# The opening of a two-layer hybrid trunk as a list of steps, with 28 identity products ahead of it, moved gate steps, and a later bias sum

## The chip, the cores and the metric

One core of a Trainium2 chip runs the whole program. The metric is the device time of one execution in microseconds (us); lower is better. The kernel before takes 2284.15 us (median of 3 runs, 2282.27 to 2289.24). The engines are called by the profile's names: PE is TensorE's matmul stream and PEld its weight loads, DVE is VectorE, ACT is ScalarE, POOL is GpSimd, SP is SyncE, which issues all large transfers.

## What is computed

The input is a sequence of 1024 rows of 1024 numbers, a conditioning vector c and integer positions. Layer A is a matrix-memory mixer (mLSTM) and a squared-ReLU MLP, layer B latent attention and an MLP. Cut to what the change touches:

```python
c_act = silu(c)
sh1, sc1, g1, sh2, sc2, g2 = split(c_act @ mod_w[layer] + mod_b[layer], 6)
h = rms_norm(x, g) * (1 + sc1) + sh1                   # modulate
q, k, v, o_pre, i_pre, f_pre = split(h @ w_in, idx)    # layer A's projections
bc = cumsum(log_sigmoid(f_pre))                        # gates, per chunk of the recurrence
y = (sigmoid(o_pre) * rms_norm(hh, head_norm)) @ w_out # hh: what the mLSTM gives
x = x + g1 * rms_norm(y)                               # residual
ckv, k_rope = split(modulate(rms_norm(x), shift, scale) @ w_dkv)   # layer B's latent K/V
qa = modulate(rms_norm(x), sh1, sc1) @ w_qa            # layer B's latent q
cos, sin = rope_tables(positions)
```

All of it is float32. A product of two matrices is made of three TensorE products of rounded parts: each factor is split into a high part (`whi`, `hTh`, `uh`, `tbh`, a copy on ACT) and a remainder (`wlo`, `hTl`, `ul`, `tbl`, a subtraction on DVE), and `mm3` adds high x high, remainder x high and high x remainder (lines 168, 169 and 170 before).

## The kernel before

The sequence is cut into eight tiles of 128 rows (`tb`), the model width into eight slices of 128 columns (`k`). The kernel writes instructions in program order; a scheduler with a timeline model then sets the order on each engine, within the dependences, the tile pools, and pins that the kernel writes by hand: `self.behind(PE, V, S)` puts what follows behind the last instruction so far of these engines, and `issue_after` behind one given instruction. All large tiles (raw weights, their parts, activations, slabs, modw rows) come from one pool of 52 units, and a transfer waits on SP until its unit is free. PSUM has two double tiles `MM` (1024 columns) and four single ones `SM` (512 columns).

**The opening** makes the first half of layer A: the first four tiles of x are normed, transposed (`transposes`, L208: TensorE products with the identity), modulated and split, and meet two groups of weights: the first of the three pieces of v with the gate columns (`value(k)`, four tiles of 344 columns, 12 products per k) and the first two heads of q (`query(h, k)`, 3 products of 512 columns per k). The modulation needs shift and scale columns, c_act @ mod_w. They come two slices at a time from a slab of mod_w (slabs 0, 2, 4, 6, each in four units): for slab 0 as a row on TensorE (`mod_row`, L1040) that ACT copies, for slabs 2, 4 and 6 as sums of eight multiples on DVE (`mod_sum`, L1030 and L1032); small TensorE products with a column of ones (`mod_cols`, L1051) then turn them into columns, and `turned` transposes x and modulates (L985 on ACT, L987 on DVE). The order of these steps is written as nested `behind` blocks. In it the four value sums live in SM tiles, the transposed x and the two heads in the two MM tiles.

**After the opening** come the second half of the first two pieces, with the late constants (`lcols`, 32 columns transposed from small rows), then the rope tables (`rope_tables`, from `posi`, cast to `posf`, transposed), and the gates (`gates`, a generator: each `yield` lets other work be written in between; L1337 and L1352 are its TensorE steps between DVE ones). Beside them run the modulation vectors for later (`mods`, one accumulation of a modw row per step, L290 and L292, then `column`: eight transposes of `acc`).

**The mLSTM's end** makes sigmoid of the output gates (L1231, ACT) and multiplies it by `headg`, a slice of `lcols`.

**Layer B's latent projections** are made beside layer A's second MLP half. Their weights are scaled by the modulation's scale when they are split; the shift's part is a bias row: DVE adds up shift x weight (`lbias`, L1549), and one product with a matrix of ones (L1552) sums it over the partitions and spreads it, written at the end of the split of each of the two weights (320 and 384 columns). `latent_mix` makes the two projections of a tile and adds the bias (L1579). The MLP's residual adds there are on POOL (L445).

Of the kernel before, what the change touches and what calls it, by code (L numbers as in the profile page):

```python
# [13 lines left out]
AF = mybir.ActivationFunctionType  # L14
# [7 lines left out]
P = 128  # L22
# [43 lines left out]
class Trunk:  # L66
# [144 lines left out]
    def consts(self):  # L211
# [11 lines left out]
        self.transposes(ps, [crow])  # L223
        c = self.C("ccol", [P, KD])
# [28 lines left out]
    def late_consts(self):  # L253
# [20 lines left out]
        self.headg = self.lcols[:, 8:16]  # L274
# [668 lines left out]
    def layer_a(self):  # L943
# [60 lines left out]
        xs, slabs, sums, accs = [], [], {}, {}  # L1004
# [17 lines left out]
        def mod_sum(k, r0=0, r1=KD):  # L1022

            if r0 == 0:
                accs[k] = self.U("acc")[:, : 4 * P].rearrange("p (s c) -> p s c", s=2)
            acc = accs[k]
# [6 lines left out]
            for j in range(2):  # L1033
                sums[k + j] = acc[:, :, j * P : (j + 1) * P]

        def mod_row(k):

            ps = self.SM()
            for i in range(KD):
                PE.matmul(ps[0:1].rearrange("p (s c) -> p s c", s=2), self.cact[:, i : i + 1], slab_part(k, i), start=i == 0, stop=i == KD - 1)  # L1040
            row = self.U("acc")[0:1, : 4 * P]
            S.copy(row, ps[0:1])
            for j in range(2):
                sums[k + j] = row.rearrange("p (s c) -> p s c", s=2)[:, :, j * P : (j + 1) * P]

        def mod_cols(k, ps):

            for j in range(2):
                acc = sums.pop(k + j)
                for s in range(2):  # L1050
                    PE.matmul(ps[:, 2 * s + j : 2 * s + j + 1], acc[:, s], self.ones[: acc.shape[0], 0:1], start=True, stop=True)  # L1051
# [5 lines left out]
        def turned(k):  # L1057

            for j in range(2):
                ps = turn[:, j * 512 : j * 512 + 512]  # L1060
                if j == 0:
                    mod_cols(k, turn[:, 512:])
                self.transposes(ps, [x[:, (k + j) * P : (k + j + 1) * P] for x in xs[:4]])
                modulate(k + j, ps, self.U("t")[:, :512], *hT_part(0, k + j, slice(0, 512)), True)
# [34 lines left out]
        w, wq, acc = [], [], [None] * 4  # L1099

        def value(k):
            for tb in range(4):
                if k == 0:
                    acc[tb] = self.SM()
# [3 lines left out]
        def query(h, *ks):  # L1108
            for k in ks:
                c = tuple(u[:, k * P : (k + 1) * P] for u in wq[h])  # L1110
                self.mm3(heads[:, h * 512 : h * 512 + 512], c, self.hT_half(hT, 0, k), k == 0, k == KD - 1)

        normed(xs[:4], 2)
        with self.behind(V, S):
            w.append(self.take(("v", 0, 0)))
            with self.behind(V, S):
                mod_sum(2, 0, 2)
                mod_row(0)
                turn, heads = self.MM(), self.MM()
                with self.behind(V):  # L1120
                    turned(0)
        mod_sum(2, 2)
        wq.append(self.take(("q", 0)))
        value(0)
        with self.behind(PE, V, S):
            turned(2)
        with self.behind(PE, V, S):
            value(1)
            w.append(self.take(("v", 0, 1)))
            wq.append(self.take(("q", 1)))  # L1130
            with self.behind(V):
                mod_sum(4)
            value(2)
            value(3)
        with self.behind(PE, V, S):
            turned(4)
        with self.behind(PE, V, S):
            query(0, 0, 1, 2, 3)
            query(1, 0, 1, 2, 3)
            w.append(self.take(("v", 0, 2)))  # L1140
            with self.behind(V):
                mod_sum(6)
            value(4)
# [833 lines left out]
```

## Time and profile before

| what | before |
|---|---|
| median of 3 runs | 2284.15 us (2282.27 to 2289.24) |
| profiled execution's own time | 2283.3 us |
| its span | 2281.5 us |
| PE busy | 2199.2 us (96%) |
| DVE busy | 1693.9 us (74%) |
| ACT busy | 1031.2 us (45%) |
| POOL busy | 473.2 us (21%) |
| opening, to the first product of v's second piece | 74.04 us |

The span is what lies between the first and the last instruction of one profiled execution; some 2 us of its time lie around it. A row of the waits names the instructions that waited, by engine, tile and line, and the instruction whose end released them, then the total, the number and the longest of these waits. A row of the windows gives one stretch: its length, then for each engine the busy time and in brackets the instructions, the granted clock of TensorE (1.00 is full), the share of the DMA engines and GB/s. A row of the groups gives line, engine, operation, tiles and shapes, number, then busy time and mean ns of one, then idle time before them. A row of the timeline gives start, duration, engine, line and tiles; matmuls overlap, so a duration there is longer than the distance to the next.

### The profile page before, as it was taken

To read this page: it belongs to the slowest core of one execution; us is meant where nothing else is said; L and a number is where in the kernel's file an instruction comes from. 1 tells how busy PE (TensorE), PEld (TensorE's weight loads), DVE (VectorE), ACT (ScalarE), POOL (GpSimd) and SP (SyncE) were. 2 spreads that over 40 slices of the span, in tenths; PEclk is the share of its full clock that TensorE was granted. 3 is DMA by queue.
4 is the path that set the end of the run, shared out by engine and by line. 5 is a ranking of instruction groups with operands and counts; after the bars stand their busy time and mean duration, and the time that the engine had idled before them with its cause. 6 is when DMAs were issued, how large, how long until landed. Compare 5 with 4: busy or idle time off the path is not lost.

```text
span 2281.5 us, 28823 instructions
## 1 busy us (share of the span) xinstructions
PE 2199.2 (96%) x10746; PEld 1833.2 (80%) x10746; DVE 1693.9 (74%) x2496; ACT 1031.2 (45%) x1708; POOL 473.2 (21%) x317
## 2 busy tenths in 40 slices
PE   6999999999999999999999999999999999999998
PEld 4988888887778877777799989988787888777776
DVE  5577687667987767878978676664678877687888
ACT  3421367564444464333344544555734444633322
POOL 0000110004543333331011000000054433333300
PEclk7999999999999999999999999999999999999999
DMA  8287443234874464454322000022357645545452
GB/s 297 71 271 261 152 131 120 88 107 131 260 237 152 153 196 145 134 171 132 123 75 59 13 17 12 29 84 102 110 158 229 193 141 189 171 134 160 130 173 104
DMA packets 300068, 320.16 MB, mean 140 GB/s; under 512 B 16041, under 2 KB 252185, under 8 KB 299929
## 3 DMA queue, kind: packets, MB, share of 16 engines
q1 hardware_dynamic: 299928, 318.33, 44.2%
q8 instruction: 84, 1.38, 0.2%
q14 instruction: 56, 0.45, 0.1%
HBM read 245.85 MB, written 72.43 MB: 140 GB/s over the span
## 4 chain that ended last, share of the span: by engine, by line
PE 77%; DVE 14%; ACT 3%; issue 3%; DMA 3%; SPq 1%; POOL 0%; DVEq 0%; ACTq 0%; POOLq 0%
PE mm L168 14%; PE mm L169 14%; PE mm L170 14%; PE sm L168 10%; PE sm L170 9%; PE sm L169 9%; PE sm L208 3%; DVE wlo L598 2%; DVE ul L807 2%; DVE y L813 2%; DMA modw<-in_mod_w_dram 1%; DVE x L733 1%; DVE y L879 1%; DVE acc L292 0%; PE mm L1847 0%
## 5 line engine op out<-in xcount | busy, mean ns | idle before, releaser
L168 PE MATMUL mm<-whi,uh 128*128 128x512 f32 x688 | 273.7, 398 | 15.4 <-DVE y L813 15.1
L169 PE MATMUL mm<-wlo,uh 128*128 128x512 f32 x688 | 271.0, 394 | 0.0
L170 PE MATMUL mm<-whi,ul 128*128 128x512 f32 x688 | 270.5, 394 | 0.0
L813 DVE TENSOR_TENSOR y<-y,mm 128x1024 f32<-128x1024 f32 (+1 forms) x161 | 192.6, 1208 | 84.9 <-PE mm L170 84.8
L625 POOL TENSOR_TENSOR tt<-raw,tt 128x512 f32<-128x512 f32 x60 | 113.6, 1893 | 610.2 <-DVE wlo L598 610.2
L168 PE MATMUL sm<-hSh,whi 128*128 128x512 f32 x560 | 221.8, 396 | 9.2 <-DVE x L733 9.2
L169 PE MATMUL sm<-hSl,whi 128*128 128x512 f32 x560 | 220.4, 394 | 0.0
L170 PE MATMUL sm<-hSh,wlo 128*128 128x512 f32 x560 | 219.3, 394 | 0.0
L733 DVE TENSOR_TENSOR x<-x,sm 128x512 f32<-128x512 f32 x198 | 132.3, 682 | 55.9 <-PE sm L170 52.9
L168 PEld LDWEIGHTS mm<-whi,uh 128*128 128x128 f32 x688 | 129.1, 188 | 55.2 <-DVE y L813 22.7
L807 DVE TENSOR_TENSOR ul<-u,uh 128x896 fp32r<-128x896 f32 (+1 forms) x120 | 153.5, 1318 | 24.8 <-ACT uh L801 24.8
L605 POOL TENSOR_TENSOR tt<-raw,raw 128x512 f32<-128x512 f32 x32 | 63.9, 1997 | 488.8 <-ACT x L740 456.9
L801 ACT CAST uh<-u 128x896 fp32r<-128x896 f32 (+1 forms) x120 | 109.6, 948 | 122.1 <-DVE ul L807 114.0
L170 PEld LDWEIGHTS mm<-whi,ul 128*128 128x128 f32 x688 | 129.2, 188 | 30.2
L169 PEld LDWEIGHTS mm<-wlo,uh 128*128 128x128 f32 x688 | 129.2, 188 | 28.9
L598 DVE TENSOR_TENSOR wlo<-raw,whi 128x1024 fp32r<-128x1024 f32 x104 | 147.6, 1420 | 5.6 <-ACT whi L594 5.6
L168 PEld LDWEIGHTS sm<-hSh,whi 128*128 128x128 f32 x560 | 105.1, 188 | 36.7 <-DVE x L733 7.9
L736 ACT ACTIVATE x<-x 128x1024 f32<-128x1024 f32 x64 | 67.8, 1059 | 143.3 <-DVE x L733 143.2
L594 ACT CAST whi<-raw 128x1024 fp32r<-128x1024 f32 x104 | 108.7, 1046 | 43.7 <-DMA raw<-in_ffn_w_dram 21.5
L170 PEld LDWEIGHTS sm<-hSh,wlo 128*128 128x128 f32 x560 | 105.1, 188 | 25.0
L169 PEld LDWEIGHTS sm<-hSl,whi 128*128 128x128 f32 x560 | 105.2, 188 | 24.2
L292 DVE SCALAR_TENSOR_TENSOR acc<-modw,cact,acc 128x1024 f32<-128x1024 f32 x84 | 114.5, 1363 | 5.3 <-DMA modw<-in_mod_w_dram 3.7
(423 smaller groups left out, 5751.9 us busy)
## 6 DMA issues: line engine op xcount, KB each, us to landing
raw<-in_ffn_w_dram SPq DMA_DIRECT2D x144, 512.0 KB
u<-us SPq DMA_DIRECT2D x112, 448.0 KB
us<-x SPq DMA_DIRECT2D x92, 512.0 KB
modw<-in_mod_w_dram SPq DMA_DIRECT2D x80, 512.0 KB
x<-xn SPq DMA_DIRECT2D x24, 512.0 KB
x<-x SPq DMA_DIRECT2D x24, 512.0 KB
x<-in_x_dram SPq DMA_DIRECT2D x16, 512.0 KB
slab<-in_mod_w_dram SPq DMA_DIRECT2D x32, 256.0 KB
```

The source lines that it names most:

```text
L168: mm(out, a[0], b[0], start=start, stop=False)
L169: mm(out, a[0], b[1], start=False, stop=False)
L170: mm(out, a[1], b[0], start=False, stop=stop)
L208: self.PE.transpose(out[: s.shape[-1], j * P : j * P + s.shape[0]], s, self.ident[: s.shape[0], : s.shape[0]])
L292: self.V.scalar_tensor_tensor(out=acc, in0=t, scalar=self.cact[:, k : k + 1], in1=acc, op0=ALU.mult, op1=ALU.add)
L594: S.copy(x[0], u)
L598: V.tensor_tensor(out=x[1], in0=u, in1=x[0].bitcast(F32), op=ALU.subtract)
L625: G.tensor_tensor(out=t1, in0=b21, in1=t2, op=ALU.subtract)
L733: V.tensor_tensor(out=dst, in0=src, in1=ps, op=ALU.add)
L801: S.copy(x[0], u)
L807: V.tensor_tensor(out=x[1], in0=u, in1=x[0].bitcast(F32), op=ALU.subtract)
L813: V.tensor_tensor(out=dst, in0=dst, in1=ps, op=ALU.add)
```

## The change

Six things are changed.

1. Behind the transposition of c's row, 28 products of the identity with itself are written into an SM tile that nothing reads.
2. The opening becomes one list of steps, each pinned behind the one before on PE, VectorE and ScalarE. In it two of the eight rows of slab 2 are summed on TensorE (`mod_row, 2, 6`), so that `sums[2]` has two accumulators; `mod_sum` is cut into pieces with other steps between; transposing (`turn`) and modulating (`made`) are separate steps; weight splits are steps. The value sums live in the MM tiles, the heads and the transposed x in SM tiles. Two raw weights are kept ahead instead of three afterwards (`early`).
3. The rope tables are written before the second half of v's first piece, not after it. `mod_steps` begins inside that loop, and `gates` has two more `yield`s and starts beside the second half of the first head.
4. The sigmoid of the output gates is written as 0.5 (1 + tanh(x/2)): ACT makes tanh, DVE adds 1 and multiplies by `headg`, which is now half of the slice of `lcols`. The number of activation table loads in ACT's stream goes from 20 to 6.
5. The product that sums `lbias` is written in `latent_mix`, behind the products of the first tile's projection that needs it, and no longer in the split of the weight.
6. The eight residual adds in layer A's MLP go from POOL to VectorE.

The core of the diff:

```diff
         self.transposes(ps, [crow])
+        busy = self.SM()
+        with self.behind(self.PE):
+            for _ in range(28):
+                self.PE.matmul(busy[:, :P], self.ident, self.ident, start=True, stop=True)
...
-        self.headg = self.lcols[:, 8:16]
+        self.headg = self.C("headg", [P, KD])
+        self.V.tensor_scalar(out=self.headg, in0=self.lcols[:, 8:16], scalar1=0.5, scalar2=None, op0=ALU.mult)
...
+        def mod_row(k, r0=0, r1=KD):
+            ps = self.SM()[0:1]
+            for i in range(r0, r1):
+                PE.matmul(ps.rearrange("p (s c) -> p s c", s=2), self.cact[:, i : i + 1], slab_part(k, i), start=i == r0, stop=i == r1 - 1)
+            row = self.U("acc")[0:1, : 4 * P]
+            S.copy(row, ps)
+            sums[k].append(row.rearrange("p (s c) -> p s c", s=2))
+        def mod_cols(k):
+            ps = self.SM()
             for j in range(2):
                 for s in range(2):
+                    for i, acc in enumerate(sums[k]):
+                        PE.matmul(
+                            ps[:, 2 * s + j : 2 * s + j + 1], acc[:, s, j * P : (j + 1) * P], self.ones[: acc.shape[0], 0:1],
+                            start=i == 0, stop=i == len(sums[k]) - 1,
+                        )
...
+        def turn(*ks):
+            for k in ks:
+                turned[k] = self.SM()
+                self.transposes(turned[k], [x[:, k * P : (k + 1) * P] for x in xs[:4]])
+        def made(k):
+            modulate(k, turned.pop(k), self.U("t")[:, :512], *hT_part(0, k, slice(0, 512)), True)
...
+        both = [self.MM() for _ in range(2)]
+        acc = [both[tb // 2][:, tb % 2 * 512 : tb % 2 * 512 + 512] for tb in range(4)]
...
+        for step in (
+            (mod_row, 0), (mod_cols, 0), (turn, 0, 1), (split_v, 0), (mod_sum, 2, 0, 2), (made, 0), (mod_sum, 2, 2, 4), (made, 1),
+            (value, 0), (mod_row, 2, 6), (value, 1), (mod_sum, 2, 4, 6),
+            (mod_cols, 2), (turn, 2, 3), (split_q, 0), (split_v, 1), (query, 0, 0, 1), (made, 2), (split_q, 1), (made, 3),
+            (value, 2), (mod_sum, 4), (value, 3), (query, 0, 2, 3), (query, 1, 0, 1),
+            (mod_cols, 4), (turn, 4, 5), (split_v, 2), (query, 1, 2, 3), (mod_sum, 6, 0, 3), (made, 4), (mod_sum, 6, 3, 5), (made, 5),
+            (value, 4), (value, 5), (mod_sum, 6, 5), (query, 0, 4, 5),
+            (mod_cols, 6), (turn, 6, 7), (query, 1, 4, 5), (made, 6), (made, 7),
+            (value, 6), (value, 7), (query, 0, 6, 7), (query, 1, 6, 7),
+        ):
+            with self.behind(PE, V, S):
+                step[0](*step[1:])
...
-        self.ahead, self.early = 3, 3
+        self.rope_tables()
+        self.ahead, self.early = 3, 2
...
         for tb in range(4, NT):
             values(tb, proj_piece(w, tb))
+            if tb > 4:
+                mod_steps(2)
+        steps = self.gates(gi, gf)
         for h in range(2):
+            next(steps)
             put_qk("q", q, h, 1, self.proj_half(self.SM(), wq[h], hT, 1))
-            next(steps)
-            mod_steps(3)
...
-                S.activation(dst, ps[:, pr * 256 : (pr + 1) * 256], AF.Sigmoid)
-                V.tensor_scalar(out=dst, in0=dst, scalar1=self.headg[:, j : j + 1], scalar2=None, op0=ALU.mult)
+                S.activation(dst, ps[:, pr * 256 : (pr + 1) * 256], AF.Tanh, scale=0.5)
+                V.tensor_scalar(out=dst, in0=dst, scalar1=1.0, scalar2=self.headg[:, j : j + 1], op0=ALU.add, op1=ALU.mult)
...
-                    if k0 + nk == KD:
-                        ps = self.SM()
-                        PE.matmul(ps[:, :n], self.ones, bias, start=True, stop=True)
-                        S.copy(bias, ps[:, :n])
...
+            if o not in self.lb:
+                bias = self.lb["bias"][:, o : o + n]
+                total = self.SM()
+                with self.tc.issue_after(self.last()):
+                    self.PE.matmul(total[:, :n], self.ones, bias, start=True, stop=True)
+                self.S.copy(bias, total[:, :n])
+                self.lb[o] = bias
...
-            xn = self.residual(y, st["g"], st["x"].pop(tb), self.G)
+            xn = self.residual(y, st["g"], st["x"].pop(tb))
```

What that does to the order of instructions is shown at three places; the line numbers of the changed kernel differ from those of before.

TensorE's first rows in the changed kernel (crow is c's row, rows the norm weights and biases, slab the first slab of mod_w, acc_275 ACT's copy of the row of sums, x_126 the first tile of x):

```order
L208 MATMUL sm_82<-ident,crow 128x8
L228 MATMUL sm_84<-ident 128x128 x28
L208 MATMUL sm_137<-ident,rows_134 128x64
L208 MATMUL sm_143<-ident,rows_140 128x96
L1044 MATMUL sm_266<-slab_146,cact 1x512 x2
L1044 MATMUL sm_266<-slab_147,cact 1x512 x2
L1044 MATMUL sm_266<-slab_148,cact 1x512 x2
L1044 MATMUL sm_266<-slab_149,cact 1x512 x2
L1055 MATMUL sm_277<-ones,acc_275 128x1 x4
L208 MATMUL sm_284<-ident,x_126 128x128
```

The 28 products are new; the other rows stand as before, where the row of sums has L1040 and the column sums L1051.

VectorE in the changed kernel, where the last slices of x's second half are modulated (L993 and L119 on t, hTh, hTl), the late constants arrive (lcols, headg), and the rope tables begin (posi, posf, pos, sin):

```order
L993 TENSOR_SCALAR t_811<-sm_806,modcol 128x512
L119 TENSOR_TENSOR hTl_766<-t_775,hTh_765 128x512
L255 COPY lcols<-sm_846 128x32
L119 TENSOR_TENSOR hTl_813<-t_811,hTh_812 128x512
L993 TENSOR_SCALAR t_831<-sm_826,modcol 128x512
L280 TENSOR_SCALAR headg<-lcols 128x8
L1467 CAST posf<-posi 8x128
```

The cast of the positions now stands here; on TensorE its transposition (sm_853<-ident,posf) is the row right behind that of lcols (sm_846), ahead of all products of v's second half. Before, the cast stood behind those pieces.

TensorE where the second bias sum of layer B stood before (mm_9349 and mm_9667 are a tile of the MLP, lbias the bias, sm_9203 the first latent projection):

```order
L169 MATMUL mm_9349<-wlo_8658,uh_9097 128x512
L168 MATMUL mm_9667<-whi_8657,uh_9097 128x512
L169 MATMUL mm_9667<-wlo_8658,uh_9097 128x512
L1552 MATMUL sm_9183<-lbias_8973,ones 128x384
L168 MATMUL sm_9203<-whi_8971,tbh_9147 128x320
L169 MATMUL sm_9203<-wlo_8972,tbh_9147 128x320
```

And in the changed kernel, at the end of that projection's 24 products:

```order
L169 MATMUL sm_9245<-wlo_9047,tbh_9192 128x320
L170 MATMUL sm_9245<-whi_9046,tbl_9193 128x320
L1570 MATMUL sm_9270<-lbias_9021,ones 128x320
L208 MATMUL sm_9287<-ident,xn_9167 128x128 x4
L208 MATMUL sm_9294<-ident,xn_9167 128x128 x4
```

The 320 columns' bias sum follows the projection; that of 384 columns follows the 24 products of the second projection, 29 rows further on.

More of the change, by code (lines that the diff above doesn't have):

```diff
@@ L1002, in values @@
             put_v(tb, 0, ps, 8, VP - 8)
-        xs, slabs, sums, accs = [], [], {}, {}
+        xs, slabs, sums, turned = [], [], {k: [] for k in range(0, KD, 2)}, {}
         def load_xs(t0, t1):
@@ L1024, in mod_sum @@
             if r0 == 0:
-                accs[k] = self.U("acc")[:, : 4 * P].rearrange("p (s c) -> p s c", s=2)
-            acc = accs[k]
+                sums[k].append(self.U("acc")[:, : 4 * P].rearrange("p (s c) -> p s c", s=2))
+            acc = sums[k][0]
             for i in range(r0, r1):
@@ L1032, in mod_sum @@
                     V.scalar_tensor_tensor(out=acc, in0=slab_part(k, i), scalar=c, in1=acc, op0=ALU.mult, op1=ALU.add)
-            for j in range(2):
-                sums[k + j] = acc[:, :, j * P : (j + 1) * P]
-        def mod_row(k):
-            ps = self.SM()
[L1039 to L1049, printed above, removed]
-                for s in range(2):
-                    PE.matmul(ps[:, 2 * s + j : 2 * s + j + 1], acc[:, s], self.ones[: acc.shape[0], 0:1], start=True, stop=True)
+        def mod_row(k, r0=0, r1=KD):
[7 more added lines that the diff above has]
+            ps = self.SM()
+            for j in range(2):
+                for s in range(2):
+                    for i, acc in enumerate(sums[k]):
[3 more added lines that the diff above has]
+                        )
+            del sums[k]
             ks = slice(k, k + 2)
@@ L1108, in query @@
         def query(h, *ks):
+            if len(heads) == h:
+                heads.append(self.SM())
             for k in ks:
                 c = tuple(u[:, k * P : (k + 1) * P] for u in wq[h])
-                self.mm3(heads[:, h * 512 : h * 512 + 512], c, self.hT_half(hT, 0, k), k == 0, k == KD - 1)
-        normed(xs[:4], 2)
[L1114 to L1143, printed above, removed]
@@ L1144, in layer_a, with split_v, split_q @@
-        with self.behind(PE, V, S):
-            turned(6)
-        with self.behind(PE):
-            value(5)
-            query(0, 4, 5)
-            query(1, 4, 5)
-            value(6)
-            value(7)
-            query(0, 6, 7)
-            query(1, 6, 7)
+                self.mm3(heads[h], c, self.hT_half(hT, 0, k), k == 0, k == KD - 1)
+        def split_v(g):
+            w.append(self.take(("v", 0, g)))
+        def split_q(h):
+            wq.append(self.take(("q", h)))
+        normed(xs[:4], 2)
@@ L1154, in layer_a @@
         w1 = [self.take(("v", 1, g)) for g in range(3)]
+        for h in range(2):
+            put_qk("q", q, h, 0, heads[h])
         for tb in range(4):
             values(tb, acc[tb])
-        for h in range(2):
-            put_qk("q", q, h, 0, heads[:, h * 512 : h * 512 + 512])
         normed(xs[4:], 0)
@@ L1174, in layer_a @@
         )
-        for tb in range(4, NT):
-            values(tb, proj_piece(w, tb))
-        steps = self.gates(gi, gf)
-        next(steps)
-        self.rope_tables()
         def mod_steps(n):
@@ L1183, in mod_steps @@
                 next(mods, None)
+        for tb in range(4, NT):
+            values(tb, proj_piece(w, tb))
+            if tb > 4:
+                mod_steps(2)
+        steps = self.gates(gi, gf)
         for h in range(2):
+            next(steps)
             put_qk("q", q, h, 1, self.proj_half(self.SM(), wq[h], hT, 1))
-            next(steps)
-            mod_steps(3)
         for p in (1, 2):
@@ L1335, in gates @@
         yield
+        yield
         ps = self.SM()
@@ L1349, in gates @@
         V.tensor_copy(p3[:, :, 1:NT], m3[:, :, 0 : NT - 1])
+        yield
         yield
```

14 lines of the change are left out of this document (2 added, 12 removed).

## The prediction

> **What bounds the kernel now.** I read the engine table of the page, the clock row, the waits of TensorE, and the opening in stretches.
>
> ```profile
> PE 2199.2 (96%) x10746; PEld 1833.2 (80%) x10746; DVE 1693.9 (74%) x2496; ACT 1031.2 (45%) x1708; POOL 473.2 (21%) x317
> PEclk7999999999999999999999999999999999999999
> ```
>
> TensorE is busy 2199.2 of 2281.5 us: 82.3 us of idle time are all that any reordering can win, plus time at a low clock. The clock row has its one weak slice at the very start.
>
> ```profile
> PE mm L1051 <- DVE acc L1032: 3.6, 1, 3.6
> PE mm L208 <- ACT t L985: 3.6, 4, 0.9
> PE sm L1552 <- DVE lbias L1549: 3.1, 1, 3.1
> PE sm L208 <- DVE acc L292: 2.2, 1, 2.2
> PE sm L1337 <- DVE gate L1328: 2.1, 1, 2.1
> PE sm L208 <- DVE gt L1465: 1.9, 1, 1.9
> PE mm L208 <- DVE modcol L1054: 1.0, 4, 0.3
> PE sm L1352 <- DVE gate L1344: 0.9, 1, 0.9
> ```
>
> Columns: total wait, times, longest. Each is a TensorE wait at a place that the change rewrites: lines 1, 2 and 7 are the opening (8.2 us; with 0.7 for the copied row of sums, 8.9), line 3 the latent bias in layer A's MLP, lines 4, 5 and 8 the gates (5.2 us), line 6 the end of the mLSTM.
>
> ```profile
> 23.00:24.00 1.00, 0.69 (x5) 0.42 (x4) 0.93 (x4) 0.00 (x0) 0.00 (x0) 0.92 1.19 280
> 24.00:37.00 13.00, 10.99 (x43) 10.51 (x44) 7.24 (x12) 7.66 (x11) 0.00 (x0) 0.50 1.10 349
> 38.00:44.00 6.00, 3.46 (x22) 3.17 (x21) 5.79 (x8) 0.00 (x0) 0.80 (x8) 1.00 1.08 375
> 46.00:54.00 8.00, 6.87 (x23) 5.53 (x24) 3.18 (x7) 3.46 (x5) 0.00 (x0) 0.50 0.53 189
> 140.00:143.00 3.00, 3.00 (x13) 2.63 (x12) 2.81 (x6) 1.04 (x1) 0.00 (x0) 0.50 0.92 318
> 1143.00:1146.00 3.00, 3.00 (x11) 2.66 (x10) 1.68 (x5) 0.48 (x1) 1.19 (x1) 0.50 0.00 0
> ```
>
> Stretches of the span; the third number from the right is the granted clock; a value between 0.5 and 1 dates a change inside a stretch (0.92 in 23 to 24: at 23.7 or so). The opening has two half-clock stretches (24 to 37, 46 to 54); in the first VectorE is busy only 7.24 of 13, so TensorE's speed sets the pace, and in 38 to 44 VectorE is busy 5.79 of 6 while TensorE waits. Behind the idle gaps at 139 and 1142 the clock is half again. The timeline of TensorE, with the wait ahead of each run of products in brackets:
>
> ```profile
> 10.18 0.72 PE L208 MATMUL sm<-ident,rows 64*128 64x64 f32 x2 [7.54 <-DMA rows<-in_norm_g_dram]
> 11.64 9.68 PE L1040 MATMUL sm<-slab,cact 128*1 128x512 f32 x16 [0.75 <-DMA slab<-in_mod_w_dram]
> 23.29 0.66 PE L208 MATMUL mm<-ident,x 128*128 128x128 f32 x4 [0.26 <-DVE modcol L1054]
> 45.08 1.87 PE L1051 MATMUL mm<-ones,acc 128*128 128x1 f32 x8 [3.62 <-DVE acc L1032]
> 74.04 0.32 PE L168 MATMUL sm<-whi,hTh 128*128 128x344 f32 x1
> 74.19 0.32 PE L169 MATMUL sm<-wlo,hTh 128*128 128x344 f32 x1
> ```
>
> The last two rows are the first products of the next piece: the opening ends at 74.04.
>
> **The change, part by part.**
>
> (A) The opening. Work of TensorE between the sums of row 0 and 74.04, from these groups:
>
> ```profile
> L168 PE MATMUL sm<-whi,hTh 128*128 128x344 f32 x37 | 13.0, 366 | 0.0
> L1032 DVE SCALAR_TENSOR_TENSOR acc<-slab,cact,acc 128x512 f32<-128x512 f32 x21 | 15.8, 751 | 0.6
> L119 DVE TENSOR_TENSOR wlo<-raw,whi 128x1032 fp32r<-128x1032 f32 (+2 forms) x8 | 9.0, 1140 | 5.5 <-ACT whi L118 5.5
> L119 DVE TENSOR_TENSOR hTl<-t,hTh 128x512 fp32r<-128x512 f32 x8 | 5.5, 690 | 9.6 <-ACT hTh L118 9.6
> ```
>
> At full clock a value product (344 wide) follows the last after 0.157 us (74.04, 74.19 and on), a query product (512 wide) after 0.157 x 512 / 344 = 0.23, a transpose after 0.107 (the four at 23.29: 0.66, less 0.23 of passage). 96 x 0.157 + 48 x 0.23 + 32 x 0.107 + four sets of column sums at about 1 us (1.87 in the half-clock row at 45.08) is 33.5 us. From 21.98 to 74.04 are 52.1: 8.2 of waits, the remaining 10.4 is the low clock.
>
> The 28 products stand behind crow's transposition. I count two instructions each, as the row of sums has 16 for its 8, at the transpose's 0.107 us full and 0.213 half: 6.0 to 11.9 us from 2.5 on. In the row of sums the clock rose at 16.9, after 5 us of dense work, and the later changes (23.7, 37.4, 44.2, 54.4) lie on a grid of 3.41 us; so it should rise at about 6.7 and the products end near 10.6, and at 14.4 if it never rises. Cover until 10.18 is the wait for the norm rows (7.54 us); the excess costs 0.4, at worst 2.8 against the slab's 11.64. In exchange the 16 sum products run at 0.427 instead of partly 0.853: 6.8 instead of 9.68 us, ending near 18.6.
>
> From there I follow the hand-made list. The sums of columns 0 at 19.3, value(0) from 22.3, column sums 2 near 28.8 (their list now has two accumulators, 16 small products for 8: 0.95 us more). Two of the 24 slab sums move to TensorE, 1.5 us less for VectorE. Then VectorE is the chain: from 20 on it owes about 18.5 us up to the end of mod_sum(4) (six weight and activation remainders at 1.14 and 0.69, four sums of slab 2, eight of slab 4 at 0.75) and about 3 us of waits on the splits: 41.5, against 45.0. Slab 6 with its remainders is 8.8 more, with one wait 51.5, against 59.3. Behind it TensorE has column sums, eight transposes, value(6), value(7) and six queries, 9.5 us: the opening ends near 61.4, 12.6 us sooner. From this I take 0.4 for the late products, 1 for handovers between engines, and for the clock 2.2: after the row of sums come about 1.5 us of waits in a window of 3.4 (a window with 0.93 us of waits was followed by half clock at 23.7), so that I expect one half-clock stretch near 20 to 27 with a chance of 0.7 (2.5 us), and a second at 42 to 48 at a half (1 us). **9.0**; the bounds are 4 (VectorE's pace as before) and 13.
>
> [...]
>
> (B) The gates and the tables. With more steps of other work in between, the transposes of gates come 98 instead of 51 TensorE rows behind those of the gate inputs: 48 products at 0.23 and 48 at 0.157, 18.6 us. Before, that chain took 14.0 us (109.5 to 123.5), 6.2 of them VectorE's rope tables (costliest group below), which move ahead; seven accumulations of mod_w rows (L292) move in, three of them ahead of the first gate operation.
>
> ```profile
> L1493 DVE SCALAR_TENSOR_TENSOR sin<-n,sin 128x256 f32<-128x256 f32 x3 | 1.3, 426 | 0.1
> L292 DVE SCALAR_TENSOR_TENSOR acc<-modw,cact,acc 128x1024 f32<-128x1024 f32 x84 | 114.5, 1363 | 5.3 <-DMA modw<-in_mod_w_dram 3.7
> SPq L287 <- PE sm L170: 18.2, 3, 12.2
> L1475 DVE CAST posf<-posi 8x128 f32<-8x128 int32 x1 | 0.2, 204 | 0.0
> 93.53 0.19 DVE L250 COPY lcols<-sm 128x32 f32<-128x32 f32 x1
> ```
>
> 14.0 - 6.2 + 7 x 1.36 is 17.3 us against 18.6: no wait, if the mod_w rows are there. They may not be: SyncE's loads (third row, 95 to 140) stood 18.2 us for buffers that TensorE frees, once for 12.2. I keep 1.5 us for that. Gone: 2.1 + 0.9 + 2.2 and the clock stretch behind 139, 1.7 (half of 3.4). New: the transposition of posf moves to the place right behind lcols and needs VectorE's cast, which stands behind hTl, t and headg (0.68 + 0.81 + 0.2 after 93.64): TensorE, in order, holds all value pieces behind it from 93.6 to 95.5: −1.9. Sum 6.9 − 1.5 − 1.9: **+3.5**, bounds −2 and +6.5.
>
> (C) Sigmoid as tanh, and the last stage.
>
> ```profile
> L1231 ACT ACT_TABLE_LOAD x7 | 9.0, 1283 | 0.1
> 280.00:380.00 100.00, 99.78 (x541) 85.89 (x540) 79.83 (x184) 67.81 (x157) 14.55 (x10) 1.00 0.42 117
> ```
>
> Fourteen table loads of ACT go, seven of them in this group, but TensorE is busy 99.78 of 100 us there: hidden, nothing. If any of it shows, then in the end's 1.9 (gt) and in ACT's 0.8 before it: **+0.6**, bounds −1 and +2.5.
>
> (D) The bias sum. Before, the 384-wide bias's product stands ahead of the whole first latent projection and waits 3.1 us for VectorE. Now 24 products (3.5 us at 0.145, scaled from 0.157 by 320/344) come ahead of it, then 320's product, eight transposes and 24 products of 384 (4.2 us): the bias that was ready at 1142.2 is asked for near 1148. 3.1 goes, and the half clock of 1142.2 to 1145.6 (1.7); the copy through ACT and the read behind it add at most 0.4, behind which the four-buffer pool has other tiles: **+4.4**, bounds 3 and 5.
>
> (E) Eight residual adds of the MLP go from POOL to VectorE.
>
> ```profile
> L445 POOL TENSOR_TENSOR xn<-xn,x x8: 2373/2396/2442, 1125.1 to 1208.6; 128x1024 f32<-128x1024 f32 x8
> 1162.30 2.37 DVE L182 SCALAR_TENSOR_TENSOR rst<-rsy,rsv 128x1 f32<-128x1 f32 x1
> 1164.70 0.16 DVE L186 SCALAR_TENSOR_TENSOR rsy<-rst,rsy 128x1 f32<-128x1 f32 x1
> 482.97 1.22 DVE L445 TENSOR_TENSOR xn<-xn,x 128x1024 f32<-128x1024 f32 x1
> 1150.00:1210.00 60.00, 59.99 (x372) 57.56 (x371) 49.64 (x163) 29.77 (x94) 13.02 (x10) 1.00 0.21 71
> ```
>
> On VectorE the add takes 1.22; on POOL 2.4, and a one-column VectorE instruction beside it lasts 2.37 where its like last 0.16. So VectorE loses 1.22 and gets back about as much. TensorE is busy 59.99 of 60: **0**. Without that cover it would be 8 x 1.22 = 9.8 us, spread over waits; bounds −2 and +1. [...]
>
> The sum is 9.0 + 3.5 + 0.6 + 4.4 + 0 = 17.5, from the profiled execution's 2283.3: 2265.8. The median of the runs, 2284.15, lies 0.85 higher: **2266.5**.
>
> **The rivals.**
>
> - *The clock holds once it has risen.* For it: a wait of 3.65 us in the MLP was followed by no low stretch. Against it: 23.7 and 139. Without the 2.2 for the clock: 2264.
>
> ```profile
> 680.95 0.50 PE L168 MATMUL sm<-hSh,whi 128*128 128x512 f32 x1 [3.65 <-DVE x L733]
> 681.00:685.00 4.00, 4.00 (x18) 3.25 (x18) 3.90 (x6) 1.02 (x1) 0.00 (x0) 1.00 0.43 110
> ```
>
> - *VectorE's slab sums keep their pace.* If mod_sum(6) ends near 55 instead of 51.5, since remainders wait for ACT's splits (15 us of idle time ahead of L119 in the opening), the opening gains 4 to 5: 2271. Against it: in 24 to 37 VectorE was idle for 5.8 us.
> - *The gates wait anyway.* The mod_w rows come late, VectorE stands before them in order, and the gate operations queued behind them come 4 to 6 us late, so that (B) ends near −2: 2272. For it: the 12.2 and the 3.7 us in the rows above. Against it: the loads move ahead with the steps.
> - *The low clock holds through the whole opening.* If the new order never fills a window of 3.41 us, 33.5 us of work take 62 (0.29 for 0.157), the waits shrink to 2: from 22 to 87, 13 late instead of 9 early, with (B), (C), (D) as forecast: 2284.15 + 13 − 8.5 = 2289. It decides from 8.5 us of loss on. Against it: before, the clock rose in the first dense window each time (37.4, 54.4).
>
> **How the numbers follow.** The forecast has 0.38 (2261 to 2270), the holding clock 0.18, the slab sums 0.20, the gates 0.19, the low clock 0.05. The runs shown spread by 0.3%, so a shift below 6.9 us counts as none: the bound is 2277.3. Of the forecast 0.97 lie below it, of the second all, of the slab sums 0.85, of the gates 0.70: 0.37 + 0.18 + 0.17 + 0.13 = 0.85 faster; 0.12 within; 0.03 slower, all of it from the low clock, whose loss has to pass 15.4 us for that. The range is 2255 to 2277: below, (A) at 13, (B) at 6.5 and (C) at 2.5 would together give 2256; above, the slab sums and the gates' price together give 2277.
>
> **What would show it.** Right: products of the identity from 2.5 to near 10.6, the row of sums over by 18.6, the next piece's first product near 65 instead of 74.04, the waits at 123, 128, 139 and 1142 gone, a new one of about 1.9 us behind posf, and VectorE's small instructions near 1162 at 0.16. Wrong: the row of sums beginning later than 12, half clock through most of 20 to 60, or the 3.1 us of lbias standing at another place.

## The result, and the profile after

The changed kernel takes 2260.28 us (median of 4 runs, 2259.39 to 2260.82) against 2285.48 us for the kernel before (4 runs, 2282.27 to 2289.24): a ratio of 0.9889, 95% interval 0.9872 to 0.9906. The forecast was 2266.5 in a range of 2255 to 2277: the time lies inside, 6 us below the forecast. The profiled executions differ by 23.5 us of span (2281.5 and 2258.0).

The engine table and the clock row of the changed kernel's page:

```profile
PE 2200.4 (97%) x10814; PEld 1835.6 (81%) x10814; DVE 1689.3 (75%) x2503; ACT 1013.2 (45%) x1695; POOL 458.1 (20%) x309
PEclk9999999999999999999999999999999999999999
```

TensorE is busy as long as before (2200.4 for 2199.2), with 9.3 us of products of the identity in it; its idle time went from 82.3 to 57.6 us, and the weak first slice of the clock row is gone.

The timeline of TensorE at the start (start, duration, engine, line, tiles, count; the wait ahead in brackets), and where the late constants and the positions are transposed:

```profile
2.44 9.29 PE L228 MATMUL sm<-ident 128*128 128x128 f32 x56
12.10 7.03 PE L1044 MATMUL sm<-slab,cact 128*1 128x512 f32 x16
19.79 1.05 PE L1055 MATMUL sm<-ones,acc 1*128 1x1 f32 x8 [0.66 <-ACT acc L1046]
82.66 0.24 PE L208 MATMUL sm<-ident,rows 32*128 32x32 f32 x1
84.70 0.22 PE L208 MATMUL sm<-ident,posf 8*128 8x8 f32 x1 [1.80 <-DVE posf L1467]
```

The products are 56 instructions and end at 11.7; the row of sums takes 7.03 us for 9.68; the late constants come at 82.66 for 93.25. All waits of TensorE between 80 and 420 us (total, times, longest) are now these:

```profile
PE sm L208 <- DVE posf L1467: 1.8, 1, 1.8
PE sm L208 <- DVE gf L1003: 0.3, 1, 0.3
PE mm L169 <- DVE wlo L119: 0.3, 1, 0.3
PE sm L208 <- DVE gt L1457: 0.2, 1, 0.2
```

The waits at the gates (2.1, 0.9, 2.2) are gone, that for gt is 0.2 for 1.9, and the new one behind posf is there. Between 1100 and 1200 one row is left, where the 3.1 us for lbias stood:

```profile
PE sm L208 <- DVE rsv L179: 0.5, 2, 0.3
```

The same instruction in both profiles dates what each stage gained. In the stage column a minus is time gained; a wait that ends at a mark counts in the row of that mark, so the 0.8 us for num before the first transposition of hn, which the prediction put to (C), stands in the row of (B):

| instruction of TensorE | before | after | difference | in this stage | forecast |
|---|---|---|---|---|---|
| transposition of lcols' rows | 93.25 | 82.66 | -10.6 | -10.6 | -9.0 (A) |
| transposition of the gate inputs | 109.51 | 100.60 | -8.9 | +1.7 | +1.9 (B, posf) |
| first transposition of hn | 386.96 | 368.38 | -18.6 | -9.7 | -5.4 (B, the rest) |
| first product of the output projection | 391.84 | 370.48 | -21.4 | -2.8 | -0.6 (C) |
| first product of layer A's MLP | 492.12 | 471.01 | -21.1 | +0.3 | 0 |
| first product of the latent q's up projection | 1221.38 | 1196.91 | -24.5 | -3.4 | -4.4 (D, E) |
| end of the span | 2281.5 | 2258.0 | -23.5 | +1.0 | 0 |

### The profile page after: what moved, and what is told of

Its sections match the earlier page's. It is cut to its first block, busy times and chain, and to the rows that moved or that the text cites. A ratio compares the mean times of both kernels' runs of the same rounds, so it can differ in the third digit from the quotient of the medians.

```text
span 2258.0 us, 28912 instructions
## 1 busy us (share of the span) xinstructions
PE 2200.4 (97%) x10814; PEld 1835.6 (81%) x10814; DVE 1689.3 (75%) x2503; ACT 1013.2 (45%) x1695; POOL 458.1 (20%) x309
## 4 chain that ended last, share of the span: by engine, by line
PE 76%; DVE 14%; ACT 3%; issue 3%; DMA 3%; SPq 1%; DVEq 0%; POOL 0%; ACTq 0%; POOLq 0%
PE mm L168 14%; PE mm L170 14%; PE mm L169 14%; PE sm L168 10%; PE sm L169 10%; PE sm L170 10%; PE sm L208 3%; DVE wlo L604 2%; DVE ul L813 2%; DVE y L819 2%; DVE x L739 1%; DMA slab<-in_mod_w_dram 1%; DVE y L885 1%; DVE acc L298 1%; DMA modw<-in_mod_w_dram 1%
## 5 line engine op out<-in xcount | busy, mean ns | idle before, releaser
L739 DVE TENSOR_TENSOR x<-x,sm 128x512 f32<-128x512 f32 x198 | 132.3, 682 | 57.6 <-PE sm L170 54.3
```

Source lines behind the costliest of these rows:

```text
L739: V.tensor_tensor(out=dst, in0=src, in1=ps, op=ALU.add)
```

## The experiments

The theory: each part works at its own place, by the waits named in the prediction and by the clock. The main rival for the 28 products: the list alone moves the opening, and they only fill idle time. The kernel before was run again beside each group of runs; its medians lie between 2283.23 and 2285.94 us, those of the changed kernel at 2260.28 and 2260.99, so differences of 1 or 2 us between kernels of different groups are read from the profiles and not from the medians alone.

### The opening: products, list, or both

Without the products (e1, and e10 in other rounds), on the kernel before alone (e2), twice as many (e11), and the whole new opening on the kernel before (e3):

```diff
 # e1, e10: the changed kernel without
-        busy = self.SM()
-        with self.behind(self.PE):
-            for _ in range(28):
-                self.PE.matmul(busy[:, :P], self.ident, self.ident, start=True, stop=True)
 # e2: the kernel before with these lines; e11: the changed kernel with range(56)
 # e3: the kernel before with these lines and the changed opening, up to finish(late)
```

> The changed kernel without its 28 products of the identity; everything else as in the changed kernel. Theory (the products raise the clock early): the row of sums, 7.0 us long in the changed kernel, takes about 9.7 again and ends near 21.3 instead of 19.1; one or two more half-clock stretches of 3.4 us follow in 20 to 40; lcols is transposed 2 to 5 us later than the changed kernel's 82.6 and the time is 2262 to 2266. Rival (the list alone does it, the products only fill idle time): VectorE's sums set the pace behind 30 us, the 2.2 us are absorbed by the waits there, and the time stays within 1 us of 2260.3.

> The kernel before with the 28 products behind the transposition of c's row and nothing else. Theory (clock): the row of sums takes 7 instead of 9.68 us and the half-clock stretch of 24 to 37 (6.5 us lost) is shortened or gone: the opening ends 4 to 8 us sooner than 74.04, time 2276 to 2280. Rival (the list does it): the clock falls again at the first waits, the opening ends 0 to 3 us sooner, time 2281 to 2285.

> The kernel before with the whole new opening (28 products, list of steps, accumulators in the double tiles, two rows of slab 2 on TensorE), but gates, rope tables, sigmoid, bias sum and residual adds as before. If the parts add up by place: lcols is transposed 10 to 10.5 us sooner than 93.25, the waits at the gates (2.1, 0.9, 2.2 us) and at lbias (3.1 us) stand as before, and the time is 2274 to 2276. If the later gains of the changed kernel come from the earlier opening itself (loads and buffers that are free sooner), the gates' waits shrink too and the time is 2266 to 2271.

> The changed kernel once more, on the same chip and in the same rounds as the next two, for a comparison of the number of products: 0, 28 and 56. 2259 to 2261 if nothing but the phase of the clock's grid of 3.41 us differs between executions.

> The changed kernel without the 28 products once more. If the 2.2 to 2.7 us that its row of sums ends later reach the end of the program, it is 2.2 to 2.7 us slower than the changed kernel of these rounds; if later half-clock stretches and waits take them up, 0 to 1.2 us slower.

> The changed kernel with 56 products of the identity. They end near 17.7 instead of 11.7 (28 more at 2 x 0.107 us), so that the row of sums ends near 25 instead of 19.1. Theory (TensorE's start sets the pace of the whole opening): lcols is transposed 5 to 6 us later and the time is 5 to 6 us above the changed kernel's. Rival (VectorE's slab sums and the transfers set the pace behind 30 us): 0 to 3 us above it.

| kernel | median us (runs) | against before | lcols' transposition |
|---|---|---|---|
| e1, no products | 2261.24 (4) | 0.9893 [0.9879, 0.9908] | 85.35 |
| e2, before and products | 2285.09 (10) | 0.9995 [0.9985, 1.0005] | 89.39 |
| e3, before and the new opening | 2277.66 (5) | 0.9965 [0.9952, 0.9978] | 82.72 |
| e9, changed kernel | 2260.99 (4; 2260.72 to 2261.07) | 0.9901 [0.9887, 0.9914] | 81.57 |
| e10, no products | 2260.57 (4; 2260.22 to 2260.95) | 0.9899 [0.9884, 0.9914] | 83.03 |
| e11, 56 products | 2265.84 (5; 2264.93 to 2268.87) | 0.9924 [0.9912, 0.9937] | 88.48 |

In the total the products are worth nothing that these runs resolve: 0.4 us slower with them in the rounds of e9 to e11, 1.0 us faster in comparison of e1 with the first runs. On the kernel before alone they give 0.3 us, though lcols comes 3.9 us sooner in the profile of e2; half-clock stretches near 388, 678 and 1521, where the profile of before has none, stand against that in this execution (mean granted clock 0.990, in before 0.991). In the opening itself they do what was forecast. Timeline of TensorE without them (e1, then e10):

```profile
11.73 9.02 PE L1040 MATMUL sm<-slab,cact 128*1 128x512 f32 x14 [0.83 <-DVE rst L195]
85.35 0.24 PE L208 MATMUL sm<-ident,rows 32*128 32x32 f32 x1
```

```profile
10.97 8.32 PE L1040 MATMUL sm<-slab,cact 128*1 128x512 f32 x16 [0.84 <-DVE rst L195]
83.03 0.24 PE L208 MATMUL sm<-ident,rows 32*128 32x32 f32 x1
```

The row of sums takes 8.3 to over 9 us for 7.03, and lcols comes 1.5 us (e10 against e9) and 2.7 us (e1 against the first profile) later. With 56 products, 112 instructions, the row of sums is held back instead:

```profile
2.44 14.88 PE L228 MATMUL sm<-ident 128*128 128x128 f32 x112
17.68 7.03 PE L1044 MATMUL sm<-slab,cact 128*1 128x512 f32 x16
88.48 0.24 PE L208 MATMUL sm<-ident,rows 32*128 32x32 f32 x1
```

Against the first profile of the changed kernel the row of sums begins 5.6 us later (17.68 for 12.10) and lcols comes 5.8 later (88.48 for 82.66); against e9, where the row begins at 10.91, they are 6.8 and 6.9. The median is 4.9 us above that of e9, in the same rounds. So a late start of TensorE passes through the opening whole, and most of it reaches the end. The list pins VectorE's sums behind steps of TensorE, so they shift with it. The profile of after says which engine is the fuller one: between 20 and 82 us TensorE is busy 58.0 of 62 us and waits 0.8 us for a slab sum, while VectorE is busy 39.6 us.

Where do the 1.5 to 2.7 us of the 28 products go? Between e9 and e10 the difference stays at 1.5 us up to layer A's MLP (471.49 and 472.99), and is 0.8 us the other way at its end. There, first in the changed kernel, then in e9, e1 and e10, the waits of ACT and TensorE from 470 on:

```profile
ACT whi L556 <- DMA raw<-in_ffn_w_dram: 4.4, 1, 4.4
PE mm L168 <- ACT x L746: 1.6, 1, 1.6
```

```profile
ACT whi L556 <- DMA raw<-in_ffn_w_dram: 3.8, 1, 3.8
PE mm L168 <- ACT x L746: 1.2, 1, 1.2
```

```profile
ACT whi L552 <- DMA raw<-in_ffn_w_dram: 2.6, 1, 2.6
```

```profile
ACT whi L552 <- DMA raw<-in_ffn_w_dram: 2.5, 1, 2.5
```

ACT stands before a transfer of the MLP's weights, and the copy that TensorE waits for (L746) is queued behind it. With the products ACT waits 1.3 to 1.8 us longer there, and TensorE waits 1.2 and 1.6 us; without them TensorE does not wait. That takes up 1.2 and 1.6 of 1.5 and 2.7 us. SyncE issues the transfers of that place 1.5 and 2.8 us sooner with the products (477.96 for 479.46, 477.47 for 480.23), but the wait ends only 0.2 and 1.0 us sooner; why is open. In these four executions the clock adds to that: behind a gap of 3.6 us near 660 the half clock lasts 6.83 us in the changed kernel and in e9, and 3.41 us in e1 and e10. Where the clock's grid falls around such a gap is in the last section; e10 loses as much again near 1500, where its half clock lasts 6.83 us for 3.41 in e9.

e3 confirms part (A) by place: lcols at 82.72, as in the changed kernel, and all later waits of TensorE stand where they stood (80 to 420 us):

```profile
PE sm L208 <- DVE acc L297: 2.2, 1, 2.2
PE sm L1325 <- DVE gate L1316: 2.1, 1, 2.1
PE sm L208 <- DVE gt L1453: 1.9, 1, 1.9
PE sm L1340 <- DVE gate L1332: 0.9, 1, 0.9
```

Its total is 7.7 us below the kernel before, 10.5 us at lcols: 2.8 less than the opening gained, and a little above the 2274 to 2276 expected. The profile of e3 has half-clock stretches of 3.41 us at 114 and 674 that the profile of before does not have; at 1.7 us each they are enough for that, if the other executions of e3 have them too.

### The gates, the tables, and the modulation steps

```diff
 # e5: the changed kernel, rope tables behind the first gate step
         finish(late)
-        self.rope_tables()
...
         for h in range(2):
             next(steps)
+            if h == 0:
+                self.rope_tables()
 # e12: the kernel before with the changed lines from finish(late) to the loop over h,
 #      and the two more yields in gates
 # e8: the changed kernel, the cast of the positions right behind the opening
+        self.posf = self.C("posf", [NT, P])
+        with self.behind(V):
+            V.tensor_copy(self.posf, self.posi)
         normed(xs[4:], 0)
```

> The kernel before with only the rope tables, the modulation steps and the gate steps moved as in the changed kernel; opening, sigmoid, bias sum and residual adds as before. If the parts add up: a wait of 1.6 to 1.9 us at the transposition of posf, none at the gates (5.2 us and 3.4 us of half clock gone), and the 2.7 us of waits at the end of the mLSTM gone too, since the modulation vectors are done earlier: 2275 to 2277. If the wait at the end of the mLSTM hangs on tanh, 2277.5 to 2279.5.

> The changed kernel with the rope tables written behind the first gate step, where they were before; the moved gate steps stay. Theory (the gates' waits went because the 6.2 us of rope tables left VectorE's gate chain): the 1.8 us wait at posf goes, but the chain is 23.5 us against 18.6 of products, so a wait of 3 to 5 us stands at the first gate transposition again, perhaps with a half-clock stretch: 2262 to 2266. Rival (the gates' waits went by the additional products in between alone): only the wait at posf goes, 2258 to 2259.

> The changed kernel with the cast of the positions on VectorE moved ahead of the norms of the second half of x, behind the opening. If the 1.8 us wait at the transposition of posf is that cast's place in VectorE's order, it goes, and lcols to the gate inputs is 1.6 to 1.8 us shorter: 2258.3 to 2259. Rival (the scheduled order moves, or the wait passes to the next VectorE result): within 0.5 us of 2260.3.

| kernel | median us (runs) | against before |
|---|---|---|
| e12, before and the gates' part | 2272.25 (4) | 0.9950 [0.9936, 0.9964] |
| e5, rope tables back | 2266.61 (4) | 0.9915 [0.9900, 0.9930] |
| e8, positions cast early | 2255.31 (4; 2254.28 to 2257.99) | 0.9868 [0.9852, 0.9884] |

e12 gains 11.0 us, more than any other part, and more than expected. All its waits of TensorE over 0.3 us between 85 and 420:

```profile
PE sm L208 <- DVE posf L1477: 0.4, 1, 0.4
PE mm L169 <- DVE wlo L119: 0.4, 1, 0.4
```

Not only the gates' waits are gone, also those at the end of the mLSTM (gt 1.9, num 0.8), with sigmoid still in place: these waits belonged to part (B), not to (C). Which of the moved steps removes them is not separated. From lcols to the first transposition of hn e12's profile takes 284.95 us, that of before 293.71, that of after 285.72; another 2.5 us of e12's profile lie ahead of lcols, where nothing was changed: there the half clock of e12 adds up to 13.65 us (38.76 to 49.00 and 59.24 to 62.65), that of before to 23.89 (23.83 to 37.49 and 44.31 to 54.55). The wait behind posf is 0.4 and not 1.8; the section on sigmoid shows why.

e5 shows why the tables had to move. Its long wait of TensorE between 80 and 130, and VectorE's timeline:

```profile
PE sm L208 <- DVE posf L1468: 8.2, 1, 8.2
```

```profile
101.77 1.28 DVE L298 SCALAR_TENSOR_TENSOR acc<-modw,cact,acc 128x1024 f32<-128x1024 f32 x1 [0.31 <-DMA modw<-in_mod_w_dram]
103.90 2.60 DVE L298 SCALAR_TENSOR_TENSOR acc<-modw,cact,acc 128x1024 f32<-128x1024 f32 x2 [0.85 <-DMA modw<-in_mod_w_dram]
106.42 0.21 DVE L1468 CAST posf<-posi 8x128 f32<-8x128 int32 x1
```

The cast stands behind six accumulations that begin at 98.1, and TensorE, in order, waits 8.2 us at its transposition. My theory named the size about right (3 to 5 us expected, 6.3 lost) and the place wrong: it is not the gates' first transposition that waits but the tables' own.

e8 takes the wait of 1.8 us away and gains 5.0 us, more than the 1.3 to 2 expected; in its profile lcols comes 0.7 us sooner, 1.2 us are the wait, 2.0 fall in layer A's MLP, where its half clock behind 658 lasts 3.41 us for 6.83. All four runs of e8 lie below all eight of the changed kernel, by 1.4 us at least, so what it gains beyond the 1.2 need not all be the luck of one execution; that stays open. It is the fastest version of this study, 0.9868 of the kernel before.

### Sigmoid or tanh

```diff
-                S.activation(dst, ps[:, pr * 256 : (pr + 1) * 256], AF.Tanh, scale=0.5)
-                V.tensor_scalar(out=dst, in0=dst, scalar1=1.0, scalar2=self.headg[:, j : j + 1], op0=ALU.add, op1=ALU.mult)
+                S.activation(dst, ps[:, pr * 256 : (pr + 1) * 256], AF.Sigmoid)
+                V.tensor_scalar(out=dst, in0=dst, scalar1=self.headg[:, j : j + 1], scalar2=None, op0=ALU.mult)
```

headg is the plain slice of lcols again.

> The changed kernel with sigmoid instead of 0.5 (1 + tanh(x/2)). Forecast (table loads lie behind full TensorE work): no row of TensorE waits more, 2259.5 to 2261. Rival (ACT's table loads made num and gt late at the end of the mLSTM): the waits of about 0.8 and 1.9 us there return, from the first transposition of hn to the output projection 2 to 2.8 us more, 2262 to 2263.5.

2257.07 us (4 runs, 2255.96 to 2258.43), 0.9874 [0.9859, 0.9888]: 3.2 and 3.9 us faster than the two medians with tanh, which neither theory expected. The waits of TensorE from 80 to 420 that differ:

```profile
PE mm L168 <- ACT sg L1220: 0.5, 1, 0.5
PE sm L208 <- DVE posf L1466: 0.4, 1, 0.4
```

Its span is 3.8 us shorter. The table loads cost 0.4 us up to the end of the mLSTM (sg), and 0.3 are lost behind 1200; the missing headg gains 1.2 us at posf, where the wait is 0.4 for 1.8; 1.0 us are in the opening and 2.3 in layer A's MLP, where the half clock lasts 3.41 us for 6.83. How long the half clock lasts there differs between executions, as above, but the four runs of e6 all lie below the eight of the changed kernel, by nearly 1 us at least, and the profile does not divide what the medians differ by. So in the profile tanh gains 0.4 us, and its halved headg costs 1.2, at a place that has nothing to do with it. VectorE's timelines, first of the changed kernel, then of e6, show how:

```profile
82.94 0.19 DVE L255 COPY lcols<-sm 128x32 f32<-128x32 f32 x1
83.65 0.81 DVE L993 TENSOR_SCALAR t<-sm,modcol 128x512 f32<-128x512 f32 x1
84.37 0.16 DVE L280 TENSOR_SCALAR headg<-lcols 128x8 f32<-128x8 f32 x1
84.44 0.21 DVE L1467 CAST posf<-posi 8x128 f32<-8x128 int32 x1
```

```profile
81.94 0.19 DVE L255 COPY lcols<-sm 128x32 f32<-128x32 f32 x1
82.05 0.20 DVE L1466 CAST posf<-posi 8x128 f32<-8x128 int32 x1
```

headg itself takes 0.16 us. What costs is the order that came with it: without headg the cast of the positions stands right behind the copy of lcols, with it behind a remainder and a modulation (0.68 and 0.81 us) as well.

### The bias sum and the residual adds

```diff
 # e4: the kernel before with the bias sum in latent_mix, as in the change
 # e7: the changed kernel with
-            xn = self.residual(y, st["g"], st["x"].pop(tb))
+            xn = self.residual(y, st["g"], st["x"].pop(tb), self.G)
```

> The kernel before with only the bias sum moved behind the first latent projections. Forecast: the wait of 3.1 us at 1142 and the half-clock stretch behind it go, 4.4 us gained, time 2280 to 2281. From the trace of the changed kernel: idle time and half clock between 1100 and 1230 together go from 8.7 to 2.0 us, so 6.7 gained, time 2277.5 to 2279.5. If it is the place of the residual adds that removes a part of this, 4 to 5 are gained here and the rest stays.

> The changed kernel with the eight residual adds of layer A's MLP on POOL again. Forecast: small VectorE instructions beside them last up to 2.4 us again, hidden behind TensorE, 2259.5 to 2261. Rival (the adds on POOL were a part of what made lbias late): idle time between 1100 and 1200 rises by 1 to 3 us, 2261.5 to 2264.

e4: 2278.11 us (6 runs), 0.9972 [0.9960, 0.9983], 7.2 us gained. e7: 2262.16 us (4 runs, 2261.28 to 2264.44), 0.9897 [0.9882, 0.9912], 1.2 to 1.9 us above the two medians of the changed kernel, as its rival had it; the ratios alone do not separate it from them (0.9889 and 0.9901). Waits of TensorE of e7 between 1100 and 1210:

```profile
PE mm L168 <- ACT whi L118: 1.1, 1, 1.1
PE mm L170 <- DVE rsv L179: 1.0, 1, 1.0
PE sm L208 <- DVE rsy L180: 0.4, 1, 0.4
```

With the adds on POOL, two of VectorE's and ACT's results are late for TensorE: 2.0 us more idle time than in the changed kernel. e4, which has the adds on POOL too, has the same rows (1.1, 0.9, 0.3), and none for lbias. Between the same two products of TensorE, that behind a wait of 1.3 us for y (at 1102.13 in before, 1084.96 in after) and the first one of the latent q's up projection, before takes 119.25 us, e4 114.22, e7 114.28 and the changed kernel 111.95: the bias alone gains 5.0 here, the adds another 2.3.

The wait put down to rsv comes about like this in e7:

```profile
1131.21 2.59 POOL L451 TENSOR_TENSOR xn<-xn,x 128x1024 f32<-128x1024 f32 x1 [1.63 <-DVE xn L450]
1131.98 2.91 DVE L813 TENSOR_TENSOR ul<-u,uh 128x1024 fp32r<-128x1024 f32 x1
1134.95 0.50 PE L170 MATMUL mm<-whi,ul 128*128 128x512 f32 x1 [0.96 <-DVE rsv L179]
```

Beside the add on POOL the subtraction ul lasts 2.91 us, in the changed kernel 1.22 (1131.30), and the product that TensorE holds is one with ul; rsv is the small instruction right behind it. Why it lasts longer there no run shows. The wait for whi is of another kind: in e7 ACT makes that copy behind ckvh, which waits for TensorE, in the changed kernel ahead of it. So a part of the price that I had set to zero is ACT's order, which changed along with the place of the adds.

## Why the prediction was right, and where it was not

- **What bounds the kernel: right.** The gain is idle time (82.3 to 57.6 us) and half clock of TensorE, nearly all of it at the places of the eight quoted waits. By medians, (A) 7.7, (B) 11.0 and (D) 7.2 us each alone on the kernel before, 1.2 to 1.9 for (E) and −3.9 to −3.2 for (C) out of the changed kernel make 23 to 25 us, against 25.2 and, in the rounds of e9, 22.2 measured: the parts add up, within what these medians resolve.
- **(A) 9.0 forecast, 10.6 in the profile, 7.7 in e3's total.** Products, row of sums and slab sums came nearly as forecast (ends 11.7 for 10.6, 19.1 for 18.6, 52.4 for 51.5). The 10.6 carried the clock's grid of before over to another execution, with a rise at 6.7; it rose at 8.3 in after and at 5.6 in e9, where the products end at 10.4. One half-clock stretch of 3.41 us came where 1.2 stretches were weighed, but at 32 instead of 20 to 27. What the prediction did not see is that the products' part of it does not last: the opening's gain is the list's (e1 and e10 are 7.9 and 10.2 us ahead of before at lcols), and what the products add there does not reach the end.
- **(B) 3.5 forecast, 8.0 in the profile (9.7 less 1.7).** The wait behind posf was forecast at 1.9 and is 1.8. Two terms were mis-sized: the reserve of 1.5 for late mod_w rows was not needed, and the half clock behind 139 was priced at 1.7, one window of the clock, where in the profile of before it lasts from 139.88 to 146.71, two windows, 3.4 us. The 0.8 for num came on top.
- **(C) 0.6 forecast, 2.8 in the profile, for a wrong reason.** The wait of 1.9 us for gt is most of that 2.8, and its cause is (B), as e12 shows; tanh gives 0.4, and headg takes back 1.2. That the table loads are hidden was right.
- **(D) 4.4 forecast, 5.0 in the stretch of e4, 7.2 in its median.** The wait for lbias is the forecast 3.1, its half clock 2.3 for 1.7 (1142.23 to 1146.82), and a wait of 0.8 for y just ahead of it went too; new waits for rsv and rsy (0.9 and 0.3), which belong to (E), go off that. What the median has beyond 5.0 no run separates.
- **(E) 0 forecast, 1.2 to 1.9 measured by e7, 2.3 in its stretch.** The step that failed is the cover (TensorE busy 59.99 of 60 up to 1210). The wait for whi stands just behind that window in the profile of before (1220.81, 1.1 us), and I had not put it to POOL; the one for rsv does not stand there at all, but in e4 and e7, where the bias sum has moved and the adds are on POOL: the cover of before is not that of the changed kernel. The sign named for VectorE came: its instructions on L182 last 0.21 us on average between 1100 and 1230, for 0.36.
- **Not forecast: +1.0 behind 1200, and 3 us lost to half clock in layer A's MLP**, where the profile of before has none at its gap of 3.65 us. Behind 1200 the profile of after has a half-clock stretch of 3.41 us at 1499.9 that before does not have; but e1 has none there and takes as long, so the cause of the 1.0 is open.
- **The bounds.** The best values of (A), (B) and (C) give 2257.6, not the 2256 of the text; 2255 as the lower end is not touched by that. The total came out 6 us below the forecast because (B), with the waits that (C) had been given, was priced too low.
- **The rivals.** The slab sums did not keep their pace, the gates did not wait, the clock did not stay low. The holding clock, with 2264, came nearest in time but not by its reason: the clock did fall, once, in the opening.

## What to carry to other kernels

Where one engine is nearly full, the waits in front of it, with the half-clock stretch that follows, can be priced one by one and summed; but check for each wait whose order makes it, since e12 removed two waits that I had put to another part. Products ahead of the work, behind which the row of sums took 7.03 us for 8.3 to over 9, are worth only what the next bound leaves of them: here waits behind a weight transfer 400 us later took up 1.2 of 1.5 and 1.6 of 2.7 us, and twice as many products cost 4.9 us. Where a tiny instruction stands in another engine's way, look at the order around it: the cast of the positions, behind 1.5 us of other work on VectorE, cost 1.2 us, the table loads behind full work 0.4.

## What the runs showed of the hardware

In the profiles of before and after the changes of the granted clock lie on one grid of 3.413 us each, to 0.01 us (before: 17.01, 23.83, 37.49, 44.31, 54.55, 139.88, 146.71, 1139.99, 1146.82, where the 1129.81 us from the first to the last are 331 times 3.4133; after: 8.28, 32.17, 35.59, 660.23, 667.05, 1499.91, 1503.32). Its offset differs from one execution to the next (3.35 us in before, 1.45 in after, 2.19 in e9, 3.38 in e10). Cut along that grid, the two profiles hold six full-clock windows with TensorE idle for 2.19 us or more (before: 40.90, 136.47, 2273.22; after: 656.81, 1496.49, 2250.84), and half clock followed each of them. Of eight with 1.42 to 1.89 us of idle time it followed one (1136.58 in before, 1.70 us); of 1291 with 1.36 us or less, two (20.42 in before with 0.92 us, 28.76 in after with none). These two hold 1.05 and 2.44 us of column sums, whose products are one column wide; four windows that hold 0.95 to 1.05 us of them kept the clock (57.97 in before; 18.52, 42.41 and 52.65 in after), so what the width does is open. Six half-clock windows with TensorE idle for 0.75 us or more were each followed by another one, of nine without idle time two were (27.25 and 139.88 in before). The windows of before around its gap of 3.65 us (these two stand 0.05 us beside the grid; on it the first is idle for 1.89 us, 55%), and of after around 3.63 us and around the column sums:

```profile
675.83:679.24 3.41, 1.47 (x7) 0.85 (x5) 3.31 (x2) 0.72 (x1) 3.33 (x3) 1.00 0.62 238
679.24:682.66 3.42, 1.71 (x7) 1.42 (x8) 3.35 (x6) 0.33 (x1) 1.46 (x1) 1.00 1.01 278
```

```profile
656.82:660.23 3.41, 0.53 (x3) 0.09 (x1) 3.36 (x3) 1.04 (x1) 3.33 (x3) 1.00 0.60 194
660.23:663.64 3.41, 2.66 (x6) 2.15 (x7) 3.37 (x5) 0.00 (x0) 0.51 (x1) 0.50 0.83 218
28.76:32.17 3.41, 3.41 (x25) 3.29 (x25) 0.16 (x1) 1.34 (x2) 0.00 (x0) 1.00 1.10 351
32.17:35.59 3.42, 3.42 (x14) 2.93 (x13) 3.40 (x5) 2.75 (x4) 0.00 (x0) 0.50 1.10 344
```

The same gap was cut into two windows with some 1.9 and 1.7 us of idle time in the profile of before, and the clock held; in the profile of after most of it fell into one (2.88 us idle) and the clock fell, for two windows, the first of them with 0.75 us of idle time. Half clock behind a gap of this length thus cost nothing in before, 1.7 us in e1 and e10 (half of 3.41) and about 3 in after (half of 6.83, less the idle time), and a comparison of two single profiles moves by this much at such a gap. Why half clock followed 1.70 us of idle time at 1136.58 in before, and not 1.89 us at 675.78, is open, and so is why the half clock behind 139 in before lasted two windows, the first of them without idle time.

How long the gap is does not order these cases by itself: 2.19 us of idle time were followed by half clock in the profile of before (136.95 to 139.14, all in one window), and 3.65 us were not.
